# The last head of Q·Kᵀ: 768 rows in one store, 256 in sixteen small ones

## The chip, the cores and the metric

The kernel runs on one core of one Trainium2 chip. The metric is the device time in microseconds of one execution. The kernel before took 1062.58 us (median of three runs, 1062.45 to 1062.63).

A core has five engines that run instructions side by side: PE (matrix multiply), ACT, DVE, POOL (GpSimd) and SP, which here only issues DMAs and waits. Data moves between the chip's large memory (HBM) and the on-chip memory of 128 partitions through 16 DMA engines, which all queues share. Matrix products land in a separate small memory (PSUM, 128 partitions of 16 KB), from which ACT or DVE copies them.

## The reference

```
q, k: (8, 12, 1024, 64) float32
out = einsum('bhid,bhjd->bhij', q, k)      # (8, 12, 1024, 1024) float32
```

For each of 96 heads the product of a 1024x64 matrix with the transpose of another gives 1024 rows of 1024 numbers: 4 MB of output per head, 403 MB in all, against 50 MB of input.

## The kernel before, in words

The 96 heads are cut into blocks of 2, 2, 4, 8 and then five times 16 heads. For every block, q and k are loaded as float32, cast to half precision by POOL (`cast_quads`, L200), and transposed (`transpose_quads`, L221, by DVE) so that the 64 features lie on partitions. Two heads of a block share the 128 partitions: one has its features on partitions 0 to 63, the other on 64 to 127. While one block's products are computed, the next is cast and transposed. The loads of the large blocks go into one tile, `x_sb` (64 KB a partition), and `input_busy` holds the event of the last cast that read it.

`scores` (L255) computes one head. Output row number 8p + t belongs to partition p, so that each partition holds eight whole neighbouring rows, 32 KB, of the output. For t = 0 to 7 PE loads 128 columns of q (every eighth, `load_weights`, L307) and multiplies them with k in two halves of 512 columns (`multiply`, L310). Two values of t (w = 2) fill half of PSUM, 128 x 2048 numbers; the ring `halves_ps` hands out the two halves in turn. ACT copies each half into an output buffer (L288), four copies per head. Then SP issues one DMA for the whole head (L302): 4 MB from 128 partitions.

The three output buffers `o_sb` go round in a ring (`outs`). ACT's first copy of a head waits until the store that last used the buffer, three heads before, has landed; `store_landing` counts that, sixteen for each store, one from each DMA engine. SP's instructions run in order, each waiting for ACT's last copy of its head. At the very end SP waits until all the stores have landed (L435), and barriers between the engines close the program.

PE and ACT also run in the order in which the program gives them instructions, waiting on semaphores only where an event asks for it. PE can run ahead of ACT by the two halves of PSUM. POOL's last work is the casting of the last block; after it, its queue is empty until the end.

Of the kernel before, what the change touches and what calls it, by code (L numbers as in the profile page):

```python
# [8 lines left out]
P = 128  # L9
# [50 lines left out]
def kernel(  # L60
# [6 lines left out]
    nc = tc.nc  # L67

    B, H, S, D = q.shape
    NT = S // P  # L70
# [4 lines left out]
    of = out.rearrange("b h i j -> (b h) i j")  # L75
# [13 lines left out]
    x_sb = pool.tile([P, NMAX * S * D // P], F32, name="x_sb", tag="x")  # L89
# [10 lines left out]
    pe = Engine(nc, nc.tensor, "pe_done")  # L100
    act = Engine(nc, nc.scalar, "act_done")
    dve = Engine(nc, nc.vector, "dve_done")
    gps = Engine(nc, nc.gpsimd, "pool_done")
    sp = Engine(nc, nc.sync, "sp_done")
# [18 lines left out]
    n, at = S * D // P * 2, 8 * S // 2  # L123
# [8 lines left out]
    input_busy = []  # L132
    outs = Ring(o_sb)
    input_landing = [Landing(nc, f"x{i}_in") for i in range(2)]
    store_landing = {id(t): Landing(nc, f"out{i}_out") for i, t in enumerate(o_sb)}

    class Block:
# [117 lines left out]
        def scores(self, n, side, regions, w):  # L255
            half, g = divmod(n, self.N // 2)
            cs = slice(half * D, (half + 1) * D)
            qT = self.qk[0].rearrange("c (g m t) -> c g t m", t=NT, m=P)
            kT = self.qk[1].rearrange("c (g j) -> c g j", j=S)
            buf, out_free, out_busy = outs.next()  # L260
            written = {}
            for u in range(NT // w):
                ps, ps_free, ps_busy = regions.next()
                first = True
                for tt in range(w):
                    stationary = qT[cs, g, w * u + tt]
                    done = pe.run(
                        lambda: load_weights(stationary, half * D),
                        self.ready if n == 0 and u == 0 else [],
                        signal=False,  # L270
                    )
                    for j in range(2):
                        at = tt * S + j * 512
                        done = pe.run(
                            lambda: multiply(
                                ps[:, at : at + 512],
                                stationary,
                                kT[cs, g, j * 512 : (j + 1) * 512],
                                half * D,
                            ),  # L280
                            ps_free,
                            signal=tt == w - 1 and j == 1,
                        )
                dst = buf[:, w * u : w * u + w].rearrange("p t j -> p (t j)")
                by_dve = w == 1 and u % 2
                copier = dve if by_dve else act
                copied = copier.run(
                    lambda: (nc.vector.tensor_copy if by_dve else nc.scalar.copy)(  # L288
                        out=dst, in_=ps[:, : w * S]
                    ),  # L290
                    out_free + [done],
                )
                written[copier] = copied
                ps_busy.append(copied)
                for do in side.get(u, []):
                    do()
            self.over = [done]
            sp.wait(written.values())
            if self.first + n == 0:
                sp.wait(blocks[EARLY].landed[0])  # L300
            dma = nc.sync.dma_start(
                out=of[self.first + n].rearrange("(p t) j -> p (t j)", p=P),  # L302
                in_=buf.rearrange("p t j -> p (t j)"),
            )
            out_busy.append(store_landing[id(buf)].start(dma))

    def load_weights(stationary, at):  # L307
        return nc.tensor.ldweights(stationary, tile_position=(at, 0))  # L308

    def multiply(dst, stationary, moving, at):  # L310
        return nc.tensor.add_instruction(  # L311
            mybir.InstMatmult(
                name=nc.get_next_instruction_name(),
                ins=[nc.tensor.lower_ap(moving), nc.tensor.lower_ap(stationary)],
                outs=[nc.tensor.lower_ap(dst)],
                start_tensor_calc=True,
                stop_tensor_calc=True,
                ldweights=False,
                tile_position=(at, 0),
                tile_size=(D, P),  # L320
            )
        )

    blocks, first = [], 0
# [4 lines left out]
    early, _, early_busy = outs.next()  # L329
    raw = early.rearrange("p t j -> p (t j)")  # L330
    at = 0
# [17 lines left out]
    def next_load(eng):  # L349
        if stream:  # L350
            b, x = stream.pop(0)
            earlier = (b.i, 0) if x else (b.i - 1, 1)
            assert b.i == EARLY or not any((i, c[0]) == earlier for i, c in casts)
            b.load(x, eng)

    for x in range(2):
# [7 lines left out]
                out=ident,  # L364
                in_=ident,
# [9 lines left out]
    def to_half(last):  # L375
        while casts:
            i, c = casts[0]
            if i > last or (blocks[i], c[0]) in stream:
                return
            if not (rooms if i == PE_BLOCKS else halves).free():  # L380
                return
            done = blocks[i].cast_quads(*c)
            if i == 2:
                early_busy[:] = [done]
            casts.pop(0)

    def transposed(b, s):
        b.transpose_quads(*s)
        to_half(b.i)

    def block(i, heads, regions, w):
        b = blocks[i]
        nxt = blocks[i + 1] if i + 1 < len(blocks) else None
        for n in heads:
            side = {}
            if nxt and nxt.by_pe:
                if n == 1:
                    side = {
                        u: [
                            lambda x=u // 2: nxt.transpose_rows(  # L400
                                x, regions.next(), dve, nc.vector.tensor_copy
                            )
                        ]
                        for u in (1, 3)
                    }
            elif nxt:
                parts = nxt.chunks()
                at = TURNS if i > EARLY else [m * b.N // len(parts) for m in range(len(parts))]
                some = [s for m, s in zip(at, parts) if m == n]
                side = {0: [lambda s=s: transposed(nxt, s) for s in some]}  # L410
            at = LOADS.get(i, {1: 1, 7: 1})
            if n in at:
                side[at[n]] = side.get(at[n], []) + [lambda: next_load(act)]
            b.scores(n, side, regions, w)
            to_half(i + 2 + (n == b.N - 1))

    for b in blocks[:PE_BLOCKS]:
# [6 lines left out]
    for x in range(2):  # L424
        blocks[0].transpose_rows(
            x, quarters.next(), (dve, act)[x], (nc.vector.tensor_copy, nc.scalar.copy)[x]
        )
        to_half(2)
    block(0, [0], quarters, 1)
    halves_ps = Ring([ps_all[:, 2 * S :], ps_all[:, : 2 * S]])  # L430
    halves_ps.busy = [quarters.busy[2] + quarters.busy[3], quarters.busy[0] + quarters.busy[1]]
    block(0, [1], halves_ps, 2)
    for i in range(1, len(blocks)):
        block(i, range(blocks[i].N), halves_ps, 2)
    sp.wait([(c, c.count) for c in store_landing.values()])  # L435


# [28 lines left out]
```

## Time and profile before

| | |
|---|---|
| median of three runs | 1062.58 us |
| the profiled execution | 1062.84 us, its span 1061.03 |
| PE busy | 700.2 us, 66% |
| ACT busy | 697.1 us, 66% |
| DVE busy | 431.0 us, 41% |
| POOL busy | 354.2 us, 33% |
| HBM read, written | 50.33 MB, 402.65 MB, 427 GB/s over the span |
| one store of a head | 4096 KB, 21.8 us from issue to landing in the median |
| one of ACT's copies | 1.86 us, 384 of them |

The span is what the profiler saw of the program; the execution's time is a little longer, and differences in the span are differences in the time. "Issue to landing" contains the time in which a store waits behind earlier ones in the queue. A row of the chain of waits says from when on, for how long and by what the end was being held up. In the windows, the DMA share is the mean over the core's 16 DMA engines, so that 0.06 is one of sixteen.

The last head's instructions stand late in the profile: ACT copies it from 1030.74 us on, SP issues its store at 1038.2, and the store's sixteen landing marks come between 1053.81 and 1059.75. The span ends at 1061.03.

### The profile page before, as it was taken

How to read it: one execution, taken by the hardware profiler on the slowest of the kernel's cores; microseconds unless marked ns; L12 is line 12 of the kernel's file. 1: busy time of each engine (PE TensorE's matmuls, PEld its weight loads, DVE VectorE, ACT ScalarE, POOL GpSimd, SP SyncE). 2: the span in 40 equal slices, each digit the busy share in tenths (PEclk: the TensorE clock that was granted, in tenths of full speed). 3: DMA queues.
4: the chain of work that ended last, by engine and by line, in shares of the span. 5: the costliest groups of instructions: out<-in, count | busy, mean ns of one | idle time of the engine just before them, and what ended most of it. 6: DMA issues, size and time to landing. Idle time of an engine off the chain costs nothing.

```text
span 1061.0 us, 3307 instructions
## 1 busy us (share of the span) xinstructions
PE 700.2 (66%) x1568; PEld 127.3 (12%) x800; DVE 431.0 (41%) x55; ACT 697.1 (66%) x386; POOL 354.2 (33%) x206
## 2 busy tenths in 40 slices
PE   6876744957477748567765856775584777778770
PEld 1111100111011101011111101111110111111110
DVE  2995939029193009339003907600761920000000
ACT  4766655857477747567756756775675777777771
POOL 7927465056380028064006509100913700000000
DMA  9999999999999999999999999999999999999997
GB/s 376 434 435 435 434 434 434 416 421 432 431 434 434 435 429 428 426 435 432 432 422 434 435 427 433 433 434 423 433 429 432 435 434 431 434 434 431 432 431 322
DMA packets 17009, 453.21 MB, mean 427 GB/s; under 512 B 1888, under 2 KB 1888, under 8 KB 2912
## 3 DMA queue, kind: packets, MB, share of 16 engines
q1 hardware_dynamic: 14976, 410.00, 89.7%
q10 hardware_dynamic: 2016, 42.99, 9.8%
q8 instruction: 9, 0.15, 0.0%
q14 instruction: 8, 0.07, 0.0%
HBM read 50.33 MB, written 402.65 MB: 427 GB/s over the span
## 4 chain that ended last, share of the span: by engine, by line
DMA 65%; ACT 16%; PE 7%; DVE 5%; POOL 4%; issue 1%; ACTq 0%; SPq 0%
DMA out_dram<-o_sb 60%; ACT o_sb L288 16%; PE ps_all L311 7%; DVE kT L229 4%; POOL half L210 3%; DMA x_sb<-in_k_dram 2%; DMA x_sb<-in_q_dram 2%; DVE qT L229 1%; DMA o_sb<-in_q_dram 0%; PE ps_all L243 0%; POOL qT L181 0%; DVE kT L250 0%; ACT kT L250 0%; ACTq L36 0%; SPq L169 0%
## 5 line engine op out<-in xcount | busy, mean ns | idle before, releaser
L288 ACT COPY o_sb<-ps_all 128x2048 f32<-128x2048 f32 (+1 forms) x384 | 694.8, 1859 | 333.5 <-DMA out_dram<-o_sb 290.2
L311 PE MATMUL ps_all<-kT,qT 64*128 64x512 f16 x1536 | 696.1, 617 | 328.6 <-ACT o_sb L288 312.8
L210 POOL CAST half<-x_sb 32x2048 f16<-32x2048 f32 x176 | 332.3, 1888 | 482.1 <-DMA x_sb<-in_q_dram 302.2
L229 DVE STREAM_TRANSPOSE qT<-half 128x2048 f16<-128x2048 f16 x22 | 202.6, 9478 | 268.1 <-POOL half L210 268.1
L229 DVE STREAM_TRANSPOSE kT<-half 128x2048 f16<-128x2048 f16 x22 | 202.5, 9539 | 137.5 <-POOL half L210 137.5
L308 PEld LDWEIGHTS <-qT 64*128 64x128 f16 x768 | 124.2, 162 | 897.4 <-issue 878.0
L229 DVE STREAM_TRANSPOSE kT<-kT 128x1024 f16<-128x1024 f16 x2 | 9.4, 4870 | 0.0
L229 DVE STREAM_TRANSPOSE qT<-qT 128x1024 f16<-128x1024 f16 x2 | 9.2, 4780 | 0.0
L210 POOL CAST qT<-o_sb 32x1024 f16<-32x1024 f32 x8 | 8.3, 1035 | 1.2 <-DMA o_sb<-in_q_dram 0.8
L210 POOL CAST kT<-o_sb 32x1024 f16<-32x1024 f32 x8 | 8.3, 1035 | 0.5
L250 DVE COPY qT<-ps_all 128x1024 f16<-128x1024 f16 x2 | 2.4, 1224 | 11.1 <-PE ps_all L243 11.1
L288 DVE COPY o_sb<-ps_all 128x1024 f32<-128x1024 f32 x4 | 4.9, 1225 | 4.4 <-PE ps_all L311 4.4
L243 PE MATMUL ps_all<-ident,qT 128*128 128x128 f16 x16 | 2.1, 311 | 6.8 <-POOL qT L181 6.7
L250 ACT COPY kT<-ps_all 128x1024 f16<-128x1024 f16 x1 | 1.0, 1012 | 4.8 <-PE ps_all L243 4.8
L181 POOL CAST qT<-o_sb 128x512 f16<-128x512 f32 x4 | 2.3, 615 | 3.7 <-DMA o_sb<-in_q_dram 3.7
L250 ACT ACT_TABLE_LOAD x1 | 1.3, 1283 | 2.8 <-issue 2.8
L250 DVE COPY kT<-ps_all 128x1024 f16<-128x1024 f16 x1 | 1.2, 1225 | 4.4 <-PE ps_all L243 4.4
L243 PE MATMUL ps_all<-ident,kT 128*128 128x128 f16 x16 | 2.0, 305 | 0.7 <-ACT o_sb L288 0.7
L181 POOL CAST kT<-o_sb 128x512 f16<-128x512 f32 x4 | 2.4, 618 | 0.3 <-DMA o_sb<-in_q_dram 0.3
L243 PEld LDWEIGHTS ps_all<-ident,qT 128*128 128x128 f16 x16 | 1.5, 141 | 7.1 <-POOL qT L181 7.1
L243 PEld LDWEIGHTS ps_all<-ident,kT 128*128 128x128 f16 x16 | 1.5, 136 | 3.3 <-POOL qT L210 1.6
L359 POOL MEMSET ident<- 128x128 f16 x1 | 0.2, 205 | 0.5 <-SPq L98 0.5
(5 smaller groups left out, 0.7 us busy)
## 6 DMA issues: line engine op xcount, KB each, us to landing
out_dram<-o_sb SPq DMA_DIRECT2D x96, 4096.0 KB, 21.8
x_sb<-in_q_dram ACTq DMA_DIRECT2D x5, 4096.0 KB, 24.1
x_sb<-in_k_dram ACTq DMA_DIRECT2D x5, 4096.0 KB, 24.3
x_sb<-in_q_dram SPq DMA_DIRECT2D x1, 2048.0 KB, 14.6
x_sb<-in_k_dram SPq DMA_DIRECT2D x1, 2048.0 KB, 19.5
o_sb<-in_k_dram ACTq DMA_DIRECT2D x4, 256.0 KB, 4.8
o_sb<-in_q_dram SPq DMA_DIRECT2D x4, 256.0 KB, 5.1
o_sb<-in_q_dram SPq DMA_DIRECT2D x1, 1024.0 KB, 8.2
```

The lines of the kernel that those rows point to most:

```text
L181: lambda: nc.gpsimd.tensor_copy(out=rows[:, :, h], in_=self.raw[x][:, h * n : (h + 1) * n].rearrange("p (r d) -> p r d", d=D),),
L210: lambda: nc.gpsimd.tensor_copy(out=dst[q0 : q0 + 32].rearrange("p (r d) -> p r d", d=32), in_=raw[32 * b : 32 * b + 32, c * m : (c + 1) * ...
L229: lambda: nc.vector.transpose(out=dst, in_=buf.rearrange("p (r i) -> p r i", i=32)),
L243: lambda: nc.tensor.transpose(t_ps[:, t], rows[:, t], ident),
L250: lambda: copy(out=dst, in_=t_ps.rearrange("c t m -> c m t")), [done]
L288: lambda: (nc.vector.tensor_copy if by_dve else nc.scalar.copy)(out=dst, in_=ps[:, : w * S]),
L308: return nc.tensor.ldweights(stationary, tile_position=(at, 0))
L311: return nc.tensor.add_instruction(mybir.InstMatmult(name=nc.get_next_instruction_name(), ins=[nc.tensor.lower_ap(moving), nc.tensor.lower ...
L359: cleared = gps.run(lambda: nc.gpsimd.memset(ident, 0.0))
```

## The change

Heads 0 to 94 are computed and stored as before. The last head goes through a new function, `scores_uneven`, which deals its 1024 rows out differently:

- rows 0 to 767: six neighbouring rows in each of the 128 partitions, in the output buffer, stored by SP in one DMA of 128 partitions by 24 KB;
- rows 768 to 847: five in each of partitions 0 to 15;
- rows 848 to 863: one in each of partitions 16 to 31;
- rows 864 to 1023: five in each of partitions 64 to 95.

The last three groups, 256 rows, are computed first. PE uses weight tiles of 32 columns for them, aimed at partitions 0 to 31 or 64 to 95 of PSUM (`at` and `to` are the row and the column of the tile in PE's array). The five rows of a partition are slots 0 to 4, and the single row is slot 5; partitions 16 to 31 get products in slots 0 to 4 as well, which are not stored. ACT copies 96 partitions by two slots at a time, three copies, into `x_sb`, waiting for `input_busy` and not for an output buffer. GpSimd waits for the third copy and then issues sixteen DMAs: for c = 0 to 3, one each from partitions 0 to 15, 16 to 31, 64 to 79 and 80 to 95, taking every fourth partition from c on. Twelve of them move four partitions by 20 KB, four move four partitions by 4 KB.

Then come the 768 rows: six products, three copies and SP's store. The final wait of SP takes in the small DMAs, which have a count of their own (`tail_landing`).

```diff
+        def scores_uneven(self, n, regions, w):
...
+            Q, even, more = 32, NT - 2, 5
+            first, single, second = P * even, P * even + Q // 2 * more, S - Q * more
+
+            def product(ps, slot, stationary, at, last):
+                m = stationary.shape[1]
+                pe.run(lambda: load_weights(stationary, half * D, at), signal=False)
+                for j in range(2):
...
+            more_sb = x_sb[: 3 * Q, : (more + 1) * S]
+            for t in range(0, more + 1, w):
+                ps = regions.next()
+                for tt in range(w):
+                    if t + tt == more:
+                        places = [(qT[:, single - Q // 2 :][:, :Q], 0)]
+                    else:
+                        places = [
+                            (qT[:, at + t + tt :][:, : Q * more - more + 1 : more], p)
+                            for at, p in ((first, 0), (second, 2 * Q))
+                        ]
+                    for i, (stationary, p) in enumerate(places):
+                        done = product(
+                            ps, tt, stationary, p, tt == w - 1 and i == len(places) - 1
+                        )
+                copied = evacuate(
+                    ps, done, more_sb[:, t * S : (t + w) * S], 3 * Q, input_busy
+                )
+            gps.wait([copied])
+            H = Q // 2
+            for c in range(4):
+                for row, p, k, col in (
+                    (first, 0, more, 0),
+                    (single, H, 1, more),
+                    (second, 2 * Q, more, 0),
+                    (second + H * more, 2 * Q + H, more, 0),
+                ):
+                    dst = head[row : row + H * k].rearrange("(p t) j -> p (t j)", t=k)
+                    self.store_part(
+                        gps,
+                        tail_landing,
+                        dst[c::4],
+                        more_sb[p + c : p + H : 4, col * S : (col + k) * S],
+                    )
+
+            buf, out_free, _ = outs.next()
+            rows = qT[:, :first].rearrange("c (m t) -> c t m", t=even)
+            for t in range(0, even, w):
+                ps = regions.next()
+                for tt in range(w):
+                    done = product(ps, tt, rows[:, t + tt], 0, tt == w - 1)
+                dst = buf[:, t : t + w].rearrange("p t j -> p (t j)")
+                copied = evacuate(ps, done, dst, P, out_free)
+            self.over = [done]
+            sp.wait([copied])
+            self.store_part(
+                sp,
+                store_landing[id(buf)],
+                head[:first].rearrange("(p t) j -> p (t j)", p=P),
+                buf[:, :even].rearrange("p t j -> p (t j)"),
+            )
+
+        def store_part(self, eng, landing, dst, src):
+            landing.start(eng.eng.dma_start(out=dst, in_=src))
...
-            b.scores(n, side, regions, w)
+            if i == len(blocks) - 1 and n == b.N - 1:
+                b.scores_uneven(n, regions, w)
+            else:
+                b.scores(n, side, regions, w)
...
-    sp.wait([(c, c.count) for c in store_landing.values()])
+    sp.wait([(c, c.count) for c in [*store_landing.values(), tail_landing]])
```

More of the change, by code (lines that the diff above doesn't have):

```diff
@@ L134 @@
     input_landing = [Landing(nc, f"x{i}_in") for i in range(2)]
+    tail_landing = Landing(nc, "tail_out")
     store_landing = {id(t): Landing(nc, f"out{i}_out") for i, t in enumerate(o_sb)}
@@ L263, in scores @@
                 ps, ps_free, ps_busy = regions.next()
-                first = True
                 for tt in range(w):
@@ L305, in scores, with evacuate @@
             out_busy.append(store_landing[id(buf)].start(dma))
-    def load_weights(stationary, at):
-        return nc.tensor.ldweights(stationary, tile_position=(at, 0))
-    def multiply(dst, stationary, moving, at):
+        def scores_uneven(self, n, regions, w):
+            half, g = divmod(n, self.N // 2)
+            cs = slice(half * D, (half + 1) * D)
+            qT = self.qk[0][cs, g * S : (g + 1) * S]
+            kT = self.qk[1][cs, g * S : (g + 1) * S]
+            head = of[self.first + n]
+            Q, even, more = 32, NT - 2, 5
[4 more added lines that the diff above has]
+                for j in range(2):
+                    col = slot * S + j * 512
+                    done = pe.run(
+                        lambda: multiply(
+                            ps[0][at : at + m, col : col + 512],
+                            stationary,
+                            kT[:, j * 512 : (j + 1) * 512],
+                            half * D,
+                            at,
+                        ),
+                        ps[1],
+                        signal=last and j == 1,
+                    )
+                return done
+            def evacuate(ps, done, dst, parts, events=()):
+                copied = act.run(
+                    lambda: nc.scalar.copy(out=dst, in_=ps[0][:parts, : w * S]),
+                    [*events, done],
+                )
+                ps[2].append(copied)
+                return copied
+            more_sb = x_sb[: 3 * Q, : (more + 1) * S]
[31 more added lines that the diff above has]
+                        more_sb[p + c : p + H : 4, col * S : (col + k) * S],
+                    )
+            buf, out_free, _ = outs.next()
[13 more added lines that the diff above has]
+                buf[:, :even].rearrange("p t j -> p (t j)"),
+            )
@@ L311, in multiply, with load_weights @@
+        def store_part(self, eng, landing, dst, src):
+            landing.start(eng.eng.dma_start(out=dst, in_=src))
+    def load_weights(stationary, at, to=0):
+        return nc.tensor.ldweights(stationary, tile_position=(at, to))
+    def multiply(dst, stationary, moving, at, to=0):
         return nc.tensor.add_instruction(
@@ L318, in multiply @@
                 ldweights=False,
-                tile_position=(at, 0),
-                tile_size=(D, P),
+                tile_position=(at, to),
+                tile_size=(D, stationary.shape[1]),
             )
```

## The prediction

> **What bounds the kernel now.** I read the page's slices and queues first, then the chain of waits, then cut the end into stretches by the view of windows, and last the timeline around the last head.
>
> ```profile
> DMA  9999999999999999999999999999999999999997
> GB/s 376 434 435 435 434 434 434 416 421 432 431 434 434 435 429 428 426 435 432 432 422 434 435 427 433 433 434 423 433 429 432 435 434 431 434 434 431 432 431 322
> q1 hardware_dynamic: 14976, 410.00, 89.7%
> ...
> DMA 65%; ACT 16%; PE 7%; DVE 5%; POOL 4%; issue 1%; ACTq 0%; SPq 0%
> ```
>
> The sixteen DMA engines are full in all 40 slices at some 430 GB/s; only the last slice falls, to 322. Nothing but less DMA work, or a better shared end, can shorten this kernel. The chain of waits in its last 50 us:
>
> ```profile
> 1008.95 21.72 DMA out_dram<-o_sb
> 1030.66 0.02 issue
> 1030.68 0.02 ACTq L36
> 1030.70 0.04 issue
> 1030.74 1.88 ACT o_sb L288
> ...
> 1034.55 3.63 ACT o_sb L288 x2
> ```
>
> ACT may copy head 95 only once the store that used the same buffer three heads before has landed, at 1030.66. The timeline there, and the windows of the end:
>
> ```profile
> 1028.49 10.06 SPq L301 DMA_DIRECT2D out_dram<-o_sb  x2
> 1030.74 3.63 ACT L288 COPY o_sb<-ps_all 128x2048 f32<-128x2048 f32 x2 [2.28 <-DMA out_dram<-o_sb]
> 1032.66 3.63 PE L311 MATMUL ps_all<-kT,qT 64*128 64x512 f16 x8 [2.29 <-ACT o_sb L288]
> ...
> 1034.55 3.63 ACT L288 COPY o_sb<-ps_all 128x2048 f32<-128x2048 f32 x2 [0.18 <-PE ps_all L311]
> ```
>
> ```profile
> 1038.20:1053.20 15.00, 0.00 (x0) 0.00 (x0) 0.00 (x0) 0.00 (x0) 0.00 (x0) 1.00 1.01 435
> 1053.20:1054.40 1.20, 0.00 (x0) 0.00 (x0) 0.00 (x0) 0.00 (x0) 0.00 (x0) 1.00 0.45 191
> 1054.40:1055.60 1.20, 0.00 (x0) 0.00 (x0) 0.00 (x0) 0.00 (x0) 0.00 (x0) 1.00 0.13 55
> 1055.60:1056.80 1.20, 0.00 (x0) 0.00 (x0) 0.00 (x0) 0.00 (x0) 0.00 (x0) 1.00 0.06 27
> 1056.80:1059.30 2.50, 0.00 (x0) 0.00 (x0) 0.00 (x0) 0.00 (x0) 0.00 (x0) 1.00 0.06 26
> 1059.30:1061.00 1.70, 0.00 (x0) 0.00 (x0) 0.00 (x0) 0.00 (x0) 0.00 (x0) 1.00 0.00 0
> ```
>
> The last column but one is the mean share of sixteen engines. From 1054.4 it is 0.13, two engines; from 1055.6 it is 0.06, one engine at 27 GB/s, until 1059.3. The trace's sixteen landing marks of the last store say it engine by engine: the first at 1053.81, their middle at 1054.6, the third last at 1055.63, then 1056.88 and 1059.75. One DMA engine is 5.1 us behind the middle and alone sets the end. That is no accident of the last store: the marks have the last engine 1.4 us behind the middle at 259 us, 2.7 at 523, 4.0 at 875. Behind 1059.75 lie 1.28 us of closing barriers.
>
> **The parts.** The profiled execution took 1062.84 us (span 1061.03, 1.81 around it), 0.26 above the median of 1062.58; I take the differences over to the median.
>
> *Less for four engines, more for twelve.* A store of 128 rows of 32 KB is 128 packets of 1.213 us in the trace, eight for each engine, so an engine moves 64 output rows (4 KB each) per head, at 0.152 us a row. After the change the 128-partition store carries 48 rows per engine in eight packets of 24 KB (8 x 0.910 = 7.28 us). The other 256 rows lie in 64 partitions: five rows in each of 48, one in each of 16. If four of these partitions belong to each engine, twelve engines get 20 rows more (68 in all) and four get 4 (52 in all). Twelve rows fewer are 12 x 0.152 = 1.82 us saved; four more cost 0.61. Each of the 16 new DMAs also marks its completion on the engines: 16 marks of 9 ns, 0.14 us.
>
> If the last engine is one of the four: its mark of head 94's store starts at 1049.60; plus 7.28, plus four rows 0.61, plus marks 0.14, plus 0.47 from the last packet to its landing gives 1058.1 instead of 1059.75: **-1.65 us**. The next engine, if it is among the twelve, goes from 1056.88 to 1057.6, the others from 1055.63 at most to 1056.4: none becomes last. If the last engine is one of the twelve, it goes to 1060.5: +0.75. The trace has no engine's name on a packet, so these are the two ends; I take the first, which is a judgement.
>
> [...]
>
> *The extra rows on PE and ACT.* They are computed first, into `x_sb`, whose last cast is long over (the page's POOL digits are 0 from the 33rd slice on), so ACT need not wait for 1030.66 with them. PE: a weight load with two matmuls takes 0.85 to 0.91 us (eight matmuls in 3.63). Eleven such products for the extra, six for the 768 rows, against eight. Tiles in different columns might overlap (0.43 each) or pay for the change of shape (0.95); I take 0.87, the row of the same 512 columns. From 1026.75 on: regions ready at 1030.3, 1033.8 and 1036.4; ACT's third copy (1.87) ends at 1038.4, GpSimd may start. The 768 rows: copies at 1038.4, 1040.2 and 1042.0, the end at 1043.8, against 1038.2 before. So SP issues the last store 5.6 us later. What covers it: the queue still holds head 94's store, whose marks come from 1044.1 to 1050.1. With 1.1 to 1.5 us from issue to first packet (SP's first loads) the fastest engines stand idle for up to 1.5 us, less what the extra DMAs give them; they have 3.4 us in hand against 1058.1, after their own 0.75. The slow engine has work until 1049.6. Cost: nothing, and about 2 us of further delay would be needed before it costs.
>
> *Sixteen DMAs from GpSimd.* Nothing else is on POOL's queue then, and nobody but SP's final wait is behind them. They start at 1038.4 and go one after another, so the last leaves at 1038.4 + 16c. No row shows POOL issuing a DMA. Below: SP's issue of a store, 0.33 us, the last at 1043.7. Above: POOL's CAST of 32x2048, 1.89 us, the last at 1068.6. I take the CAST of 32x1024, 1.035: POOL's software does a small job there too. The last issue ends at 1055.0; with some 2.2 us to landing (an estimate: 1.0 to the first packet, 0.76 for 20 KB, 0.47 to land) it lands at 1057.2, 0.9 us ahead of the slow engine. It costs nothing up to c = 1.09, eats the whole gain at 1.20, and makes 0.2% (2.1 us) slower at 1.33.
>
> *Also:* SP waits on one more semaphore at the end, under 0.1 us. PE's and POOL's extra instructions, at most one more fetch of 8 KB (0.31 us on one engine); I count none.
>
> Sum: -1.65 us, 0.16%: 1060.9.
>
> **Rivals.**
>
> *GpSimd is late.* Mechanism: the issue time c decides, from 1.09 on. At 1.3 the last lands at 1061.4 (1064.2 us in all, +0.16%), at 1.4 at 1063.0 (1065.8), at the upper bound of 1.89 at 1070.8 (1073.6). For it: one engine, sixteen in a row, and only 19.7 us between 1038.4 and 1058.1. Against it: four rows each are little to describe.
> [...]
>
> *All sixteen go through the same four engines.* A DMA of four partitions need not take the engines that a store of 128 takes. Then four engines carry 4 x (5+1+5+5) = 64 extra rows each, 9.70 us, on top of 7.28: 7.3 us more than now. An engine that landed between 1053.8 and 1055.6 would land between 1061.1 and 1062.9, 1.4 to 3.1 after 1059.75, so 1065.1 us in the middle, slower by 0.24%. It decides as soon as the four get 36 rows more than now. For it: no small DMA in the trace to the contrary.
> [...]
>
> *The slow engine is not among the four:* 1063.3, +0.07%, as worked out.
>
> *A larger gain,* over 2.1 us: the slow engine would have to lose more than its 12 rows; only if its lag shrank too.
>
> **Chances.** 0.2% is about what a measurement of this kernel can tell from no change. Forecast 0.48 (its own range 1060.5 to 1061.3); slow engine elsewhere 0.15 (1063.3); GpSimd late 0.22 (half of it below +2.1 us, the rest to 1073); the same four engines 0.09 (1065.1); larger gain 0.06. Faster by 0.2%: 0.08 with the forecast's lower edge. Slower: 0.11 + 0.08 and 0.07 for a late last store or a start-up of POOL's queue that no row shows: 0.26. Within: 0.66. The range takes 1060.2 to 1065.8: below it the rest of the larger gains, above it an issue time over 1.4.
>
> **What the new profile would show.** DMA issues from POOL at a line of their own, sixteen, the first near 1038.4 and the distance between two of them as c; ACT copies of 96x2048, three, ahead of 1038.4; SP's last store near 1043.8; in the windows of the end, a share of 0.06 lasting until about 1057.6; the last of the sixteen landing marks of the large store near 1057.5 to 1058.1. If the last marks belong to the small DMAs, GpSimd was late; if four engines are busy at the end (0.25), all went through the same four; if one engine is still busy alone until 1060, the slow one is not among the four lightened.
>
> Wrong it would be, above all, through c, through a laggard that the change doesn't lighten, or through small DMAs that don't spread.

## The result, and the profile after

The changed kernel took 1068.14 us (median of six runs, 1067.53 to 1069.12) against 1062.61 (1062.14 to 1063.73) for the kernel before in the same comparison: a ratio of 1.0052, 95% interval 1.0039 to 1.0065. It is 0.52% slower; 1060.9 was forecast.

The profiled execution took 1067.91 us with a span of 1066.13, 5.07 and 5.10 more than before. From the page of the changed kernel, the rates of the slices, the new queue and the new issues:

```profile
GB/s 375 435 433 433 436 432 432 418 420 434 433 432 433 433 427 432 422 434 433 436 424 434 433 428 431 432 436 426 432 429 434 433 432 433 432 434 431 434 433 242
q0 software_dynamic: 512, 1.05, 0.3%
L395 POOL DMA_DIRECT2D out_dram<-x_sb x16 | 8.3, 527 | 191.6 <-ACT x_sb L336 191.6
```

Thirty-nine slices are as before to within 4 GB/s; the last falls to 242 GB/s instead of 322. POOL's sixteen issues take 527 ns each, 8.30 us together. The timeline of the last head, the answer to the one shown of before:

```profile
1029.07 3.63 ACT L336 COPY x_sb<-ps_all 96x2048 f32<-96x2048 f32 x2 [0.23 <-PE ps_all L401]
...
1032.88 1.86 ACT L336 COPY x_sb<-ps_all 96x2048 f32<-96x2048 f32 x1 [0.18 <-PE ps_all L401]
...
1034.72 5.68 ACT L336 COPY o_sb<-ps_all 128x2048 f32<-128x2048 f32 x3
1035.05 8.30 POOL L395 DMA_DIRECT2D out_dram<-x_sb  x16 [191.62 <-ACT x_sb L336]
...
1040.42 0.33 SPq L395 DMA_DIRECT2D out_dram<-o_sb  x1
```

The small DMAs leave between 1035.05 and 1043.35, and SP's last store at 1040.42. Neither is late. The windows of the end (the last two columns are the mean share of sixteen DMA engines and GB/s):

```profile
1042.00:1044.00 2.00, 0.00 (x0) 0.00 (x0) 0.00 (x0) 0.00 (x0) 1.35 (x3) 1.00 1.00 395
1044.00:1046.00 2.00, 0.00 (x0) 0.00 (x0) 0.00 (x0) 0.00 (x0) 0.00 (x0) 1.00 0.98 357
1046.00:1048.00 2.00, 0.00 (x0) 0.00 (x0) 0.00 (x0) 0.00 (x0) 0.00 (x0) 1.00 0.97 367
1048.00:1050.00 2.00, 0.00 (x0) 0.00 (x0) 0.00 (x0) 0.00 (x0) 0.00 (x0) 1.00 0.96 365
...
1056.00:1058.00 2.00, 0.00 (x0) 0.00 (x0) 0.00 (x0) 0.00 (x0) 0.00 (x0) 1.00 0.28 104
1058.00:1063.00 5.00, 0.00 (x0) 0.00 (x0) 0.00 (x0) 0.00 (x0) 0.00 (x0) 1.00 0.23 97
1063.00:1066.00 3.00, 0.00 (x0) 0.00 (x0) 0.00 (x0) 0.00 (x0) 0.00 (x0) 1.00 0.00 0
```

Two things stand here. From 1056 to 1063 the share is a quarter: four engines work and twelve are done (the last of them, the slow engine of the store before, at 1058.39). The trace's 64 data packets of the small DMAs run in four chains, never more than four at a time, one chain on each of four engines, from the first small DMA to the last. The last of them lands at 1063.63; the large store's last mark came at 1058.39. And from 1044 to 1050, while all engines are busy (0.96 to 0.98), they move only 357 to 367 GB/s; this is called the dip below. Over the eight microseconds from 1042 it is 371 GB/s. Before, it was this, in the same window:

```profile
1042.00:1050.00 8.00, 0.00 (x0) 0.00 (x0) 0.00 (x0) 0.00 (x0) 0.00 (x0) 1.00 0.99 426
```

A third part lies behind the last landing. From there to the end of the span it takes 2.50 us instead of 1.28. SP's waits of the changed kernel, and the closing instruction of POOL in it:

```profile
SPq L98 <- POOLq L98: 1.2, 1, 1.2
```

```profile
L98 POOLq DRAIN  x1: 1367/1367/1367, 1063.9 to 1063.9; - x1
```

The same instruction in the kernel before:

```profile
L98 POOLq DRAIN  x1: 41/41/41, 1060.0 to 1060.0; - x1
```

So the 5.10 us are 3.88 in the last landing (1063.63 for 1059.75) and 1.22 in closing.

### The profile page after: what moved, and what is told of

It reads as the page before. It is cut to its first block, busy times and chain, and to the rows that moved or that the text cites. A ratio compares the mean times of both kernels' runs of the same rounds, so it can differ in the third digit from the quotient of the medians.

```text
span 1066.1 us, 3354 instructions
## 1 busy us (share of the span) xinstructions
PE 704.2 (66%) x1586; PEld 128.1 (12%) x809; DVE 431.0 (40%) x55; ACT 700.9 (66%) x388; POOL 362.2 (34%) x222
## 4 chain that ended last, share of the span: by engine, by line
DMA 65%; ACT 16%; PE 7%; DVE 5%; POOL 4%; issue 1%; ACTq 0%; SPq 0%
DMA out_dram<-o_sb 60%; ACT o_sb L288 15%; PE ps_all L401 7%; DVE kT L230 4%; POOL half L211 3%; DMA x_sb<-in_k_dram 2%; DMA x_sb<-in_q_dram 2%; POOL out_dram L395 1%; DVE qT L230 1%; DMA o_sb<-in_q_dram 0%; ACT x_sb L336 0%; PE ps_all L244 0%; POOL qT L182 0%; DVE kT L251 0%; ACT kT L251 0%
## 5 line engine op out<-in xcount | busy, mean ns | idle before, releaser
L401 PE MATMUL ps_all<-kT,qT 64*128 64x512 f16 (+1 forms) x1554 | 700.1, 617 | 326.9 <-ACT o_sb L288 310.8
L288 ACT COPY o_sb<-ps_all 128x2048 f32<-128x2048 f32 (+1 forms) x380 | 687.5, 1859 | 331.5 <-DMA out_dram<-o_sb 289.0
L398 PEld LDWEIGHTS <-qT 64*128 64x128 f16 (+1 forms) x777 | 125.0, 161 | 898.8 <-issue 879.6
L395 POOL DMA_DIRECT2D out_dram<-x_sb x16 | 8.3, 527 | 191.6 <-ACT x_sb L336 191.6
L336 ACT COPY x_sb<-ps_all 96x2048 f32<-96x2048 f32 x3 | 5.5, 1862 | 0.4 <-PE ps_all L401 0.4
L336 ACT COPY o_sb<-ps_all 128x2048 f32<-128x2048 f32 x3 | 5.6, 1865 | 0.1
```

Source lines behind the costliest of these rows:

```text
L336: lambda: nc.scalar.copy(out=dst, in_=ps[0][:parts, : w * S]),
L395: landing.start(eng.eng.dma_start(out=dst, in_=src))
L398: return nc.tensor.ldweights(stationary, tile_position=(at, to))
L401: return nc.tensor.add_instruction(mybir.InstMatmult(name=nc.get_next_instruction_name(), ins=[nc.tensor.lower_ap(moving), nc.tensor.lower ...
```

## The experiments

The theory after the result: each four-partition DMA runs on the same four engines, which get 64 extra rows each; besides, the small DMAs slow the others while they run, and POOL's closing drain grows with the DMAs that it has issued. The rivals: the queue does it (GpSimd's DMAs, not four partitions as such, go to the same engines or slow the others); and the slow engine of the store before is still what ends the program. Each ratio below is to the kernel before in the same comparison, with its 95% interval.

**The same sixteen DMAs from SP** (`four_by_sp`), ahead of its large store:

```diff
-            gps.wait([copied])
+            sp.wait([copied])
...
-                        gps,
+                        sp,
```

> The sixteen four-partition DMAs are issued by SP, ahead of its large store; all else as changed. Theory P (place): a DMA of four partitions runs on the same four engines whatever queue it comes from, and the closing drain of POOL (1.37 us in the changed kernel, 0.04 before) belongs to GpSimd's use of DMAs. Then four engines still carry 64 extra rows each (9.70 us behind 7.28): in the windows of the end a share of 0.25 from some 1056 on, the last landing at 1062.0 to 1063.6, 1.3 us of closing, a time of 1064.9 to 1066.6, and POOL's drain short again. Rival Q (queue): only GpSimd's queue puts everything on four engines. Then SP's DMAs spread, no share of 0.25 at the end, and a time of 1060.5 to 1062.

Measured: 1066.19 us (1065.21 to 1066.96), ratio 1.0028 (1.0017 to 1.0039). From its timeline and its windows:

```profile
1035.67 17.07 SPq L395 DMA_DIRECT2D out_dram<-x_sb  x16
1052.78 0.46 SPq L395 DMA_DIRECT2D out_dram<-o_sb  x1
```

```profile
1046.00:1050.00 4.00, 0.00 (x0) 0.00 (x0) 0.00 (x0) 0.00 (x0) 0.00 (x0) 1.00 0.48 169
1050.00:1053.00 3.00, 0.00 (x0) 0.00 (x0) 0.00 (x0) 0.00 (x0) 0.00 (x0) 1.00 0.22 94
```

Head 94's store runs out, and then a share of 0.22 at 94 GB/s remains, four engines, until the large store comes; here too the packets of the small DMAs run in four chains. So the four engines are not GpSimd's doing: four partitions go to four engines, sixteen times the same, from SP too. The time itself is no clean comparison, since SP was held up: its sixteen issues took 17.07 us, 1.07 each instead of 0.33, and the large store left 12 us later than in the changed kernel. POOL's drain was back at 41 ns and closing at 1.27 us.

**Wider DMAs.** If four partitions are the cause, DMAs of more partitions should spread. `wide16_gps` sends the same rows in four GpSimd DMAs of 16 neighbouring partitions, `wide8_sp` in eight from SP of 8, `wide15_sp` in three from SP of 15 and one of a single row.

```diff
-            for c in range(4):
+            for c in range(1):
...
-                        dst[c::4],
-                        more_sb[p + c : p + H : 4, col * S : (col + k) * S],
+                        dst[c::1],
+                        more_sb[p + c : p + H : 1, col * S : (col + k) * S],
```

The diff is that of `wide16_gps`; in `wide8_sp` the 4 becomes 2 and SP issues.

> The same 256 rows in the same partitions, stored by GpSimd in four DMAs of sixteen partitions instead of sixteen of four. Theory P: sixteen partitions go to sixteen engines, one each, so each engine has 16 rows more and 64 in all, as before the change. The slow engine ends the large store near 1059.8 to 1060.3 again, the closing stays long (2.5 us, POOL's drain over 1 us): a time of 1063.7 to 1064.6. Rival Q: GpSimd's queue uses four engines here too, and the time stays above 1066.

> The same rows in eight DMAs of eight partitions, issued by SP. Theory P: eight engines get 32 rows more (80 in all, +2.4 us against before), the other eight 48 (-2.4 us). If the slow engine is among the eight loaded: last landing near 1062.2, a time of 1064.9 to 1065.4. If it is among the other eight: it ends near 1057.4, the loaded ones at 1056.2 to 1058.2 (at 1059.3 if the second slowest is one), a time of 1060.4 to 1062.1. Rival Q (spread over all): 1062.4 to 1063.

> 255 of the 256 rows in three DMAs of fifteen partitions (six, six and five rows in a partition) and one row in a DMA of its own, issued by SP; the rows lie in other partitions of the extra tile than in the changed kernel. Theory P: fifteen engines get 17 rows more (65 in all, +0.15 us), one gets none (48, -2.4 us). If the slow engine is the one left out: the others end at 1055.8, the second slowest at 1057.0, the slow one at 1057.4: a time of 1060.1 to 1060.6. If not: the slow one ends near 1059.9, a time of 1062.5 to 1063.1.

Measured: `wide16_gps` 1066.89 (1064.32 to 1069.13), ratio 1.0037 (1.0024 to 1.005); `wide8_sp` 1066.05 (1064.99 to 1067.36), 1.0033 (1.0022 to 1.0045); `wide15_sp` 1067.19 (1065.4 to 1067.6), 1.0037 (1.0023 to 1.005). All three miss. The window of `wide16_gps`:

```profile
1042.00:1050.00 8.00, 0.00 (x0) 0.00 (x0) 0.00 (x0) 0.00 (x0) 0.00 (x0) 1.00 0.98 313
```

The time of `wide16_gps` lies where rival Q had put it, but not for Q's reason: the load did spread (up to thirteen packets of the small DMAs at a time), and the sixteen engines, busy at 0.98, moved only 313 GB/s for eight microseconds. `wide15_sp` shows the same, 272 to 320 GB/s from 1046 to 1054, with the large store issued in time, at 1040.78. So spreading alone isn't enough; something about these rows slows every engine. In `wide8_sp` SP was held for 11.44 us by its eight issues and the large store left at 1047.74; it tells nothing apart.

**A quarter of the small DMAs** (`quarter`): only c = 0, so that 192 rows are not stored.

```diff
-            for c in range(4):
+            for c in range(1):
```

> Only the first four of the sixteen small DMAs are issued (c = 0); 192 of the last head's rows are computed and not stored. Theory A: the changed kernel ends with four DMA engines that carry all sixteen small DMAs, 64 rows each behind 48. Here they carry 16 behind 48, so they end with the large store, near 1056; the slow engine is not one of them and ends at 1057.5 to 1058.4; POOL's closing drain is about 0.39 us (four DMAs; 1.37 with sixteen), the closing 1.6. A time of 1060.9 to 1061.9, 6 to 7 us below the changed kernel. Rival B: the changed kernel is late because every engine is slow behind the large store (371 GB/s from 1042 to 1054 where 430 is usual), whatever the four carry: the large store's last marks stay at 1058.4 or later and a time over 1062.5.

Measured: 1060.41 us (1059.41 to 1060.6), ratio 0.9973 (0.9963 to 0.9983). Its windows and its drain:

```profile
1042.00:1050.00 8.00, 0.00 (x0) 0.00 (x0) 0.00 (x0) 0.00 (x0) 0.00 (x0) 1.00 1.00 409
...
1053.00:1056.00 3.00, 0.00 (x0) 0.00 (x0) 0.00 (x0) 0.00 (x0) 0.00 (x0) 1.00 0.12 49
1056.00:1058.00 2.00, 0.00 (x0) 0.00 (x0) 0.00 (x0) 0.00 (x0) 0.00 (x0) 1.00 0.00 0
```

```profile
L98 POOLq DRAIN  x1: 388/388/388, 1056.8 to 1056.8; - x1
```

The stretch at a quarter is gone, and the end is again the large store's slow engine, landing at 1056.55. That is its 48 rows and none more: 7.29 us after its mark of head 94's store at 1049.26. So the slow engine is not one of the four, and it gains when its rows go elsewhere. Without the twelve DMAs the last landing is 7.08 us earlier than in the changed kernel and the drain 0.98 us shorter: what made it slow came with them. The time lies 0.5 us below what was expected.

**The place of the 256 rows.** `strided32` and `adjacent32` put them in 32 partitions, eight rows each, and store them with one GpSimd DMA. In `strided32` these are partitions 3, 7, ... 127, in `adjacent32` 0 to 31. Queue, size and number of DMAs are the same.

```diff
-            for c in range(4):
-                for row, p, k, col in (
...
+            self.store_part(
+                gps,
+                tail_landing,
+                head[first:].rearrange("(p t) j -> p (t j)", t=NT),
+                more_sb[3::4, :],
+            )
```

(`adjacent32` has `more_sb[:, :]` of a tile of 32 partitions.)

> The extra 256 rows lie as eight rows in every fourth partition (3, 7, ..., 127), computed with full-width weight tiles (four copies by ACT instead of three), and are stored by one GpSimd DMA of 32 partitions, two for each engine. Each engine carries 64 rows again. Theory A (place in SBUF): partitions that lie close together share a path into SBUF, and a DMA that draws on few such paths is slow on all engines; spread over all partitions it is not. No stretch after 1036 below 400 GB/s until some 1053, the slow engine last near 1059.8 to 1060.6, a drain of 0.13: a time of 1062.6 to 1063.6. Rival B (GpSimd's queue beside SP's slows the engines): a dip to 200 to 350 GB/s as in the kernel with DMAs of sixteen partitions, and a time over 1064.5.

> The same in partitions 0 to 31 (eight rows each), one GpSimd DMA of 32 partitions. Each engine carries 64 rows again. Theory A (place in SBUF): all 1 MB comes from one quarter of the partitions, a dip to 200 to 300 GB/s for some microseconds after 1038, the last landing at 1062 to 1065, a time over 1064.5. Rival B (the queue): the same dip as with the rows spread over every fourth partition.

Measured: `strided32` 1062.51 (1061.98 to 1062.89), ratio 0.9995 (0.9986 to 1.0005); `adjacent32` 1065.4 (1064.37 to 1066.27), ratio 1.0024 (1.0014 to 1.0033). The window of `strided32`, then that of `adjacent32`:

```profile
1042.00:1050.00 8.00, 0.00 (x0) 0.00 (x0) 0.00 (x0) 0.00 (x0) 0.00 (x0) 1.00 0.99 426
```

```profile
1042.00:1050.00 8.00, 0.00 (x0) 0.00 (x0) 0.00 (x0) 0.00 (x0) 0.00 (x0) 1.00 0.87 268
```

With the same DMA from the same queue, the rate stays at 426 GB/s, as before, from every fourth partition, and falls to 268 from 32 neighbours, where single packets of 32 KB took up to 3.7 us instead of 1.21. The rows go to the same place in HBM in both. The place in the on-chip memory does it and the queue rival falls. That a shared path lies behind it, as the expectation's theory A has it, no run shows. In `strided32` the four busy engines at the end are gone too: from 1056 to 1058 the share is 0.09, where it is 0.28 in the changed kernel. `strided32` came 0.1 us below its expected range.

`own_paths` keeps the four engines and their 64 extra rows but takes them from partitions 0 to 15 and 32 to 47, in eight GpSimd DMAs of four partitions by 32 KB. That the same four engines read these partitions in the large store was assumed; no run shows it.

```diff
+            for p in (0, Q):
+                dst = head[p * 4 : p * 4 + H * NT].rearrange("(p t) j -> p (t j)", t=NT)
+                for c in range(4):
...
+                        gps, tail_landing, dst[c::4], more_sb[p + c : p + H : 4, :]
```

> The changed kernel with its 256 extra rows (now rows 0 to 255 of the head; the 768 are the rest) in partitions 0 to 15 and 32 to 47, eight in each, stored by GpSimd in eight DMAs of four partitions by 32 KB. The four engines carry 64 extra rows each, as in the changed kernel. Theory A: the dip of the changed kernel behind 1042 (371 GB/s) comes from four engines reading partitions that belong to other engines' part of the large store; where they read only their own, there is no dip: 410 GB/s or more until some 1052, the last landing at 1061.0 to 1062.4, POOL's drain 0.7 us, a time of 1064.7 to 1066.2. Rival B: the dip comes with small DMAs or GpSimd's queue wherever the data lies: under 390 GB/s, the last landing at 1063 or later, a time over 1066.6.

Measured: 1065.97 (1064.49 to 1067.72), ratio 1.0029 (1.0019 to 1.004). Its windows and drain:

```profile
1042.00:1050.00 8.00, 0.00 (x0) 0.00 (x0) 0.00 (x0) 0.05 (x1) 0.00 (x0) 1.00 1.00 412
...
1056.00:1058.00 2.00, 0.00 (x0) 0.00 (x0) 0.00 (x0) 0.00 (x0) 0.00 (x0) 1.00 0.27 115
```

```profile
L98 POOLq DRAIN  x1: 714/714/714, 1062.5 to 1062.5; - x1
```

The four engines are alone at the end as before (0.27), but the dip is nearly gone (412 for 371 in the same window), and the last landing is at 1062.21 instead of 1063.63. It is the same load on the same number of engines, so the partitions that they read from were worth about 1.4 us of the landing. Two other things differ as well and were not tested apart: eight DMAs instead of sixteen, and the rows of the head that they carry.

**The drain** (`drain_probe`): the kernel before, with sixteen tiny loads issued by GpSimd in the middle of the program, at about 490 us.

```diff
+            if i == 5 and n == 14:
+                for c in range(16):
+                    probe_landing.start(
+                        nc.gpsimd.dma_start(
+                            out=probe[:, c * 16 : (c + 1) * 16],
+                            in_=flat[0][4 * c : 4 * c + 4, :16],
+                        )
+                    )
```

> The kernel before, with sixteen loads of 4 x 64 bytes by GpSimd added in the middle (after head 62), into a tile that nothing reads. Theory A: POOL's closing drain costs about 0.083 us for each DMA that GpSimd has issued, however long ago: a drain of 1.37 us, a time of 1063.8 to 1064.1. Rival B: it costs only for DMAs issued shortly before the end: a drain of 0.04 and 1062.5 to 1062.9.

Measured: 1064.58 (1063.26 to 1065.8), ratio 1.0015 (1.0005 to 1.0024). Its closing instruction on POOL (on another line here):

```profile
L99 POOLq DRAIN  x1: 1362/1362/1362, 1059.3 to 1059.3; - x1
```

The drain is 1362 ns although the DMAs had landed over 500 us earlier, and closing takes 2.41 us. With 41, 140, 388, 714 and 1362 to 1367 ns for 0, 1, 4, 8 and 16 GpSimd DMAs, it costs about 0.08 us a DMA, whenever it was issued. The median lies some 0.5 to 0.8 us above what the expectation allowed; where that comes from stays open.

**Where the slow engine is.** Three kernels change only SP's last store of the kernel before. `skip15` sends 128 x 6 rows, then two rows from 120 partitions and two from the last 8; `seven` sends 128 x 7 and then one row from 119, 7 and 2 partitions; `four92` sends 128 x 7 and one row from 92 and 36. `skip15` is meant to leave one engine out of the DMA of 120 partitions, `seven` to load seven engines with that of 119, `four92` to load four with that of 92. For `seven` the trace shows it: engines with some 17 packets of 4 KB each, seven for 119. For `four92` it shows engines with 23 rows more, four for 92. That the 120 partitions of `skip15` left an engine out, and how many engines took the last 36 of `four92`, no run shows; both are assumed in the ranges expected. That the engines of the small DMAs are the first in the order of the 128-partition store is assumed too; no run here shows it.

```diff
+            pieces = [(0, P, 0, 7), (0, 92, 7, 8), (92, P, 7, 8)] if self.first + n == BH - 1 else [(0, P, 0, NT)]
+            for p0, p1, t0, t1 in pieces:
+                stored = landing.start(
+                    nc.sync.dma_start(
+                        out=head[p0:p1, t0 * S : t1 * S],
+                        in_=rows[p0:p1, t0 * S : t1 * S],
+                    )
+                )
```

> [...] If the slow engine is the one left out, the last landing falls from 1059.7 to about 1057.4 and the time by 2.0 to 2.4 us, to 1060.2 to 1060.7. If not, the time stays at 1062.4 to 1063.1.

> The kernel before with SP's store of the last head cut otherwise: seven rows of all 128 partitions, then one row of partitions 0 to 118 in a DMA of 119 partitions (a multiple of 7: seven engines), of the next seven, and of the last two. By place, the first seven engines carry 74 or 75 rows (+1.5 us), the other nine 56 (-1.2 us). If the slow engine is among the nine: the last landing at 1058.5, a time of 1061.2 to 1061.7. If it is among the first seven: 1061.3, a time of 1063.9 to 1064.6.

> [...] The slow engine lies among the first seven by the run with seven engines; if it is the fifth to seventh, it ends 0.8 us sooner and the loaded four near 1058.3: a time of 1061.5 to 1062.2. If it is one of the first four: the last landing near 1062.4, a time of 1064.9 to 1065.5.

Measured: `skip15` 1063.49 (1062.33 to 1065.84), ratio 1.0008 (0.9999 to 1.0017); `seven` 1064.98 (1064.26 to 1066.31), 1.0025 (1.0014 to 1.0035); `four92` 1063.18 (1061.95 to 1064.65), 1.0004 (0.9995 to 1.0013). The end of `seven`, then that of `four92`:

```profile
1058.00:1061.00 3.00, 0.00 (x0) 0.00 (x0) 0.00 (x0) 0.00 (x0) 0.00 (x0) 1.00 0.06 25
```

```profile
1056.00:1058.00 2.00, 0.00 (x0) 0.00 (x0) 0.00 (x0) 0.00 (x0) 0.00 (x0) 1.00 0.22 90
1058.00:1061.00 3.00, 0.00 (x0) 0.00 (x0) 0.00 (x0) 0.00 (x0) 0.00 (x0) 1.00 0.02 7
```

In `seven` one engine (0.06) is busy alone to the end; its last 28 KB packet ends at 1058.31, and then it has some 17 packets of 4 KB, so it is among the seven loaded. In `skip15` it was still last, at 1061.25, so it is not the one left out, if one was. In `four92` the slow engine's last 28 KB packet ends at 1057.41 and it is not last; the last landing, 1059.24, belongs to the engines loaded with 23 rows more. So it is one of the seven and not of the four: the fifth to the seventh, if that order holds and is the same in all these DMAs. `four92` missed its expectation: the slow engine was relieved, but its four engines came to an end at almost the same time as the slow one had before, and the median shows no gain. `skip15` and `seven` came some 0.4 us above the ranges expected for what they show.

The landing marks of the kernel before show besides that this engine is not slow in the last store, but late. From its mark of head 94 to that of head 95 it took 9.67 us (1050.08 to 1059.75); the middle of the sixteen took 9.66. It carries its lag with it: over nine earlier stores the lag behind the middle grew from 4.48 us at 948 to 5.17 at 1035, some 0.08 us a store.

## Why the prediction was wrong

**The bound** was read rightly. The DMA engines, full to the last slice, and one slow engine set the end; `quarter` shows that an engine with fewer rows does end earlier (the slow one at 1056.55 instead of 1059.75). The large store's last mark went from 1059.75 to 1058.39, close to the 1058.1 of the forecast, though for another reason: the slow engine had 48 rows, not 52, and its mark of head 94 came 0.88 us later than before, at 1050.96, after the dip.

**The step that failed** is "If four of these partitions belong to each engine, twelve engines get 20 rows more (68 in all) and four get 4 (52 in all)". The partitions didn't bring engines of the large store with them: the sixteen DMAs of four each ran in four chains of packets, at a share of 0.23 to 0.28 from 1056 to 1063, so all went to the same four engines, as far as a trace without engine names can tell. The twelve others got nothing and the four got 64 rows. This is the rival "All sixteen go through the same four engines", down to the share of 0.25 that was named as its sign. It had a chance of 0.09, although no row of the trace stood for either reading; the chance should have been nearer to even.

**The rival's size was also too small**: 1065.1 against 1068.14 measured, or 1062.58 + 5.07 = 1067.65 by the two profiled executions, from which the parts here are taken. It had 2.5 us for the later landing (the middle of its own span, 1.4 to 3.1, would have been 2.25), and 3.88 came. Without the dip, by `own_paths`, it is 1062.21 - 1059.75 = 2.46, as the rival had it; the other 1.42 is put down to the slowdown of the engines by packets from neighbouring partitions, which no part of the prediction priced. That such a slowdown exists is shown by `strided32` and `adjacent32`; its size here rests on that one comparison of profiles.

**"SP waits on one more semaphore at the end, under 0.1 us"** missed the closing drain: 1.22 us, a cost of GpSimd's DMAs that the trace of before couldn't show, having none. It was priced neither in the sum nor in a rival. The three parts are the whole of the difference between the two profiles: 2.46 + 1.42 + 1.22 = 5.10. The medians differ by 5.53.

**GpSimd's issue time** was taken as 1.035 us and is 0.527. It lies between the bounds of 0.33 and 1.89, nearer to SP's issue than to the CAST that was taken as nearest. The rival "GpSimd is late", with 0.22, is false: the last issue ends at 1043.35, not 1055.0.

**The extra rows on PE and ACT** cost nothing, as said, but the times were off. ACT's third copy ended at 1034.74 and not at 1038.4, because products of 32 columns at different places ran beside each other (sixteen matmuls in 3.66 us, where eight of full width take 3.63), which was the alternative that the prediction named and didn't take. That gave SP's store 3.4 us more in hand (1040.42 for 1043.8), of which nothing came, since the store was covered either way.

**"The slow engine is not among the four"** can't be told as it was put, since the four lightened engines never came to be. The runs put it in the fifth to seventh place, if the order assumed for the small DMAs of SP holds. Whether partitions 16 to 31 of a large store are this engine's, on which the judgement turned, no run shows; in `quarter`, with 48 rows, it landed at 1056.55. Why this engine falls behind stays open.

## What to carry to other kernels

The small DMAs didn't inherit the engines of the big one whose rows they carry: sixteen of four partitions used the same four (a share of 0.23 to 0.28 at the end). Before splitting a transfer to balance the sixteen engines, put one such small DMA on the chip and read from the share in the windows how many engines it uses and whether the next one moves on. The rate of stores that ran together depended on which partitions they read from: 256 rows from every fourth partition cost nothing here (426 GB/s) and the same rows from 32 neighbours 0.24% (268 GB/s). And price GpSimd's DMAs twice, at the issue (0.527 us each here) and in POOL's closing drain (about 0.08 us each); with SP as the issuer the drain stayed at 41 ns.

## What the runs showed of the hardware that had not been expected

- POOL's closing drain grew by about 0.08 us for each DMA that GpSimd had issued in the program: 41 ns for none, 140 for one, 388 for four, 714 for eight, 1362 to 1367 for sixteen, even if they landed over 500 us earlier.
- SP's issue of a store takes 0.33 us in the kernel before; the small ones took 1.07 to 1.43 us each in `four_by_sp` and `wide8_sp` (17.07 us for sixteen, 11.44 for eight), and the large store behind them left only at 1052.78 and 1047.74. The cause was not tested by itself.
- One GpSimd DMA of 1 MB from 32 neighbouring partitions pulled the sixteen engines together down to 268 GB/s for eight microseconds; from every fourth partition it left them at 426.
- Sixteen matmuls of 64x32 tiles at two column places went through PE in 3.66 us, where eight of 64x128 take 3.63; at one column place, in `adjacent32`, eight of 64x32 took 3.63 too.
